# Decays by pairs of heads, gate products and k's decay on VectorE, smaller steps and longer stand-in matmuls in a linear-attention mixer with a feed-forward network

## The chip, the core and the metric

The kernel runs on one core of a Trainium2 chip. The metric is the time of one execution in microseconds (us) on the device. Shorter is better.

## The reference, cut to what matters

One decoder layer is computed: a gated linear attention mixer and then a gated feed-forward network with a causal convolution, each modulated by a conditioning vector c and followed by a residual and a layer norm. There are 2048 tokens, a width of 1024 and 2816 hidden units. Everything is float32.

```python
def post_norm_residual(x, cs, w_mod, b_mod, ln_gain, ln_bias, sublayer):
    shift, scale, gate = jnp.split((cs @ w_mod + b_mod)[:, None, :], 3, axis=-1)
    y = sublayer(x * (1 + scale) + shift)
    return layer_norm(DN_ALPHA * x + (1 + gate) * y, ln_gain, ln_bias)

# gla_mixer: 4 heads, keys 128 wide, values 256 wide, chunks of 64 tokens
    q, k, v, r, a_lr = split(h @ w_in)
    log_a = jax.nn.log_sigmoid(a_lr @ w_a2 + b_a) / GLA_TAU
    bcum = jnp.cumsum(chunks(log_a), axis=3)
    q_dec = qf * jnp.exp(bcum)
    k_inv = kf * jnp.exp(-bcum)
    k_dec = kf * jnp.exp(blast - bcum)
    att = jnp.where(causal, einsum(q_dec, k_inv), 0.0)
    o = einsum(att, vf) + q_dec @ state
    state = state * exp(blast) + einsum(k_dec, vf)
    return (rms_norm(o) * norm_g * jax.nn.silu(r)) @ w_o
```

## The kernel before, in words

**Products.** A float32 product is made of three TensorE matmuls in a reduced format: operands are split into a high part (a cast on ScalarE, line 104) and a low part (a subtraction on VectorE, line 107), and mm3 (lines 109 to 112) multiplies high by high, high by low and low by high. Weights come from memory as raw (512 KB), are split into hl, and hl is what TensorE reads.

**Mixer.** It goes over four blocks of 512 tokens. A block has 32 units of weights: 0 to 3 are v for heads 0 and 1; 4 to 7 are Q and K of heads 0 and 1; 8 to 11 r; 12 to 15 v for heads 2 and 3; 16 to 19 their Q and K; 20 to 23 r; 24 to 27 and 28 to 31 the two halves of the output projection. After each unit tick() runs what at_unit has put down for it: head_a to head_d (transposes of k, attention matrix, states, output of a head), and the preparation of the next block: its tokens (make_xm at unit 25, which modulates xraw at line 361 and splits it to xm), its low-rank decay input A3 (unit 28) and its decays (unit 29).

**Decays.** decays() makes for every head E1 and E2, the exponentials of the cumulated decays and of their negatives, through abs, exp and log on ScalarE and mn (lines 465, 468) and a scan (469) on VectorE. It needs another table of functions on ScalarE than silu does, so it begins with a table load (line 452), and the next silu (line 624) with another. gemm_q multiplies q by E1 (598 to 600), gemm_k multiplies k by E2 (611), splits KI (613) and then multiplies KI32 in place by el on GpSimd (616), which gives k for the state; TensorE transposes that at line 633.

**Gate.** The gate of the mixer's residual, G1, is a vector of 1024 that depends on c. gate_step adds one eighth of it (line 269, an instruction over 128 x 1024), gate_end finishes it. In blocks 0 and 1 the output projection's raw weights are multiplied by G1 (fold_G1, line 373, on GpSimd), in eight products a block, before they are split; the products are then kept in memory for the later blocks. The modulation for the feed-forward network (mod_cols(1, ...), lines 226 and 231, instructions over 128 x 512 on mraw) is made in block 0 too, two quarters of a group per step; mod2 (437 to 439) finishes it.

**End of a block.** out_proj accumulates four tiles of tokens in four banks of PSUM; z (line 746) evacuates each with the residual, and the next matmuls of that bank wait for it.

**Beginning.** TensorE first runs 32 stand-in matmuls on constants (spin, line 397), then sums up products for the modulation of the mixer's input: mod_cols adds rows 0 to 5 of c's matrix on VectorE (macc), ScalarE makes rows 6 and 7 (mpart, line 239), TensorE sums over partitions (242 and 257), more stand-ins come in between (2 and 9), and the result md (258) modulates the first tokens. ScalarE also begins the sum for the second group (line 224).

**Order.** All engines work through queues in order. Which instruction stands where is decided by a scheduler when the kernel is built, from the order of the program and its buffers; order(later, earlier) adds a constraint. All large loads are issued from one queue (SP) in order.

## Time and profile before

| | |
|---|---|
| time, median of 3 runs | 2188.53 us (2188.11 to 2189.34) |
| the profiled execution's own time | 2188.48 us |
| its span, first to last instruction | 2186.6 us |
| TensorE busy with matmuls | 2140.0 us, 98% |
| VectorE busy | 1447.3 us, 66% |
| ScalarE busy | 874.0 us, 40% |
| GpSimd busy | 191.0 us, 9% |
| mean granted clock of TensorE | 0.991 |

TensorE fills nearly the whole span. What it doesn't fill is 46.6 us; a matmul at a lower clock counts as busy, so a stretch at half the clock hides further time. The mixer takes about the first 870 us, the feed-forward network the rest.

### The profile page before, as it was taken

What the parts mean: (1) busy time and instruction counts of PE and PEld (TensorE: products, weight loads), DVE (VectorE), ACT (ScalarE), POOL (GpSimd) and SP (SyncE); (2) the same over time, 40 slices, a digit from 0 to 9 for tenths busy, and PEclk for the clock granted to TensorE, in tenths of its full rate; (3) what the DMA queues carried; (4) which work ended last, traced back from release to release, by engine and by line L of the source; (5) the groups of instructions that cost most, each with busy time, mean ns of one, the idle gap of its engine ahead of it and who ended that gap; (6) DMA issues with size and microseconds to landing.
All of it is one profiled execution on the core that took longest, in us unless ns stands there. A gap on an engine that the chain in (4) does not pass through costs nothing.

```text
span 2186.6 us, 26742 instructions
## 1 busy us (share of the span) xinstructions
PE 2140.0 (98%) x9891; PEld 1780.0 (81%) x9891; DVE 1447.3 (66%) x1998; ACT 874.0 (40%) x1326; POOL 191.0 (9%) x346
## 2 busy tenths in 40 slices
PE   8999899999999999999999999999999999999998
PEld 7788688877887888778888888888888888888887
DVE  6868864576445423688777779766666697578556
ACT  3634442353333223454444446333333443344333
POOL 0103311231010001100000000000000000011002
PEclk9999999999999999999999999999999999999999
DMA  7378357578746644688554559877777897577562
GB/s 295 135 245 294 116 202 258 187 282 346 284 182 221 237 159 174 256 323 319 188 190 171 187 184 319 313 268 260 263 256 268 273 321 283 183 240 268 193 202 87
DMA packets 150211, 515.66 MB, mean 236 GB/s; under 512 B 17120, under 2 KB 17248, under 8 KB 132160
## 3 DMA queue, kind: packets, MB, share of 16 engines
q1 hardware_dynamic: 150080, 513.94, 66.2%
q8 instruction: 78, 1.28, 0.2%
q14 instruction: 53, 0.43, 0.1%
HBM read 351.09 MB, written 162.79 MB: 235 GB/s over the span
## 4 chain that ended last, share of the span: by engine, by line
PE 86%; DVE 6%; DMA 3%; issue 2%; ACT 2%; POOL 1%; SPq 0%; DVEq 0%; POOLq 0%; ACTq 0%
PE ps_mm L110 21%; PE ps_mm L112 21%; PE ps_mm L111 20%; PE ps_w L111 7%; PE ps_w L110 7%; PE ps_w L112 7%; DMA raw<-in_wab_dram 1%; DVE macc L231 1%; DVE hl L107 1%; DVE az L469 1%; ACT hl L104 1%; PE ps_w L716 1%; DVE xm L107 0%; PE ps_w L757 0%; DVE xraw L361 0%
## 5 line engine op out<-in xcount | busy, mean ns | idle before, releaser
L110 PE MATMUL ps_mm<-xc,hl 128*128 128x512 f32 x704 | 274.3, 390 | 1.6 <-ACT p L945 0.8
L112 PE MATMUL ps_mm<-xc,hl 128*128 128x512 f32 x704 | 274.0, 389 | 0.2 <-DVE hl L107 0.2
L111 PE MATMUL ps_mm<-xc,hl 128*128 128x512 f32 x704 | 273.8, 389 | 0.0
L110 PE MATMUL ps_mm<-xm,hl 128*128 128x512 f32 x496 | 196.0, 395 | 0.0
L112 PE MATMUL ps_mm<-xm,hl 128*128 128x512 f32 x496 | 193.8, 391 | 0.4 <-DVE hl L107 0.4
L111 PE MATMUL ps_mm<-xm,hl 128*128 128x512 f32 x496 | 194.0, 391 | 0.0
L110 PEld LDWEIGHTS ps_mm<-xc,hl 128*128 128x128 f32 x704 | 132.1, 188 | 30.0 <-ACT p L945 1.5
L112 PEld LDWEIGHTS ps_mm<-xc,hl 128*128 128x128 f32 x704 | 132.1, 188 | 27.9 <-DVE hl L107 0.6
L111 PEld LDWEIGHTS ps_mm<-xc,hl 128*128 128x128 f32 x704 | 132.1, 188 | 27.4
L107 DVE TENSOR_TENSOR hl<-raw,hl 128x1024 fp32r<-128x1024 f32 (+1 forms) x91 | 107.9, 1187 | 68.0 <-ACT hl L104 67.6
L959 DVE SCALAR_TENSOR_TENSOR ct<-U,cw_sb,ct 128x512 f32<-128x512 f32 x176 | 131.7, 748 | 19.2 <-ACT ct L953 17.7
L104 ACT CAST hl<-raw 128x1024 fp32r<-128x1024 f32 (+1 forms) x91 | 89.3, 982 | 135.0 <-PE ps_mm L112 64.7
L110 PE MATMUL ps_w<-xc,hl 128*128 128x512 f32 x352 | 136.9, 389 | 0.0
L111 PE MATMUL ps_w<-xc,hl 128*128 128x512 f32 x352 | 136.9, 389 | 0.0
L112 PE MATMUL ps_w<-xc,hl 128*128 128x512 f32 x352 | 136.9, 389 | 0.0
L104 ACT CAST dhl<-raw 128x1024 fp32r<-128x1024 f32 x57 | 60.0, 1053 | 163.7 <-PE ps_mm L112 101.0
L107 DVE TENSOR_TENSOR dhl<-raw,dhl 128x1024 fp32r<-128x1024 f32 x57 | 69.6, 1222 | 69.2 <-ACT dhl L104 69.1
L110 PE MATMUL ps_mm<-hl,gated 128*128 128x512 f32 x256 | 101.9, 398 | 8.5 <-DVE z L746 8.5
L112 PEld LDWEIGHTS ps_mm<-xm,hl 128*128 128x128 f32 x496 | 93.4, 188 | 20.3 <-DVE hl L107 0.6
L110 PEld LDWEIGHTS ps_mm<-xm,hl 128*128 128x128 f32 x496 | 93.7, 189 | 19.0 <-DVE v L107 0.4
L111 PEld LDWEIGHTS ps_mm<-xm,hl 128*128 128x128 f32 x496 | 93.6, 189 | 18.1 <-issue 0.2
L110 PE MATMUL ps_mm<-hl,xm 128*128 128x512 f32 x256 | 100.6, 394 | 4.0 <-DVE z L746 4.0
(239 smaller groups left out, 5014.0 us busy)
## 6 DMA issues: line engine op xcount, KB each, us to landing
hl<-wq_d SPq DMA_DIRECT2D x64, 1024.0 KB, 4.8
hc_d<-ct SPq DMA_DIRECT2D x154, 256.0 KB, 2.5
raw<-hc_d SPq DMA_DIRECT2D x70, 512.0 KB, 4.3
draw<-wc_d SPq DMA_DIRECT2D x70, 512.0 KB, 4.6
raw<-in_wab_dram SPq DMA_DIRECT2D x64, 512.0 KB, 4.8
wq_d<-hl SPq DMA_DIRECT2D x32, 1024.0 KB, 4.9
wu<-in_wup_dram SPq DMA_DIRECT2D x44, 512.0 KB, 4.3
wg<-in_wup_dram SPq DMA_DIRECT2D x44, 512.0 KB, 3.7
```

The source lines that it names most:

```text
L104: accs["copy"] = nc.scalar.copy(h, src)
L107: return nc.vector.tensor_tensor(l, src if lsrc is None else lsrc, h.bitcast(F32), op=ALU.subtract)
L110: nc.tensor.matmul(po, a[0], b[0], start=first, stop=False, skip_group_check=resumed)
L111: nc.tensor.matmul(po, a[0], b[1], start=False, stop=False, skip_group_check=resumed)
L112: return nc.tensor.matmul(po, a[1], b[0], start=False, stop=last, skip_group_check=resumed)
L231: accs["last"] = nc.vector.scalar_tensor_tensor(acc, wk, sc, acc, op0=ALU.mult, op1=ALU.add)
L469: nc.vector.tensor_tensor_scan(az, smask, mn, 0.0, op0=ALU.mult, op1=ALU.add)
L716: nc.tensor.transpose(pt[:, s * P:s * P + P], on[:, s, e * P:e * P + P], ident)
L959: nc.vector.scalar_tensor_tensor(ct, U[:, o + i:o + i + 512], cw_sb[:, j, i:i + 1], ct, op0=ALU.mult, op1=ALU.add)
```

## The change

- **Beginning:** 62, 4 and 18 stand-ins instead of 32, 2 and 9. VectorE adds rows 0 to 6, and only row 7 is ScalarE's. The first three raw weights are loaded between the other transfers of the beginning instead of behind them.
- **Gate product and k's decay:** fold_G1 is a VectorE instruction; k's decay is one VectorE instruction over 128 x 512 with el as a broadcast operand, instead of two GpSimd instructions over 128 x 256.
- **Decays:** heads 0 and 1 at unit 29 of the block before (at the beginning for block 0), heads 2 and 3 at unit 12 of the block itself. E1 and E2 have 4 buffers instead of 8, A3 has a buffer of its own. There are eight more table loads: 16 behind the first one of the kernel where there were 8.
- **Steps:** gate steps of block 0 one unit earlier and each behind the latest split of weights; mod_cols(1, ...) in 16 steps of one quarter at units 14 to 24 instead of eight steps of two at 17 to 24.

Lines from 266 on move by one to three: 361, 373, 437, 598, 611, 746 become 362, 374, 440, 601, 614, 748, and k's decay is 618.

```diff
-SPIN = (32, 2, 9)
+SPIN = (62, 4, 18)
...
         if dk == 0:
-            nc.vector.tensor_scalar(acc, raw, cs[:, 0:1], None, op0=ALU.mult)
+            i = nc.vector.tensor_scalar(acc, raw, cs[:, 0:1], None, op0=ALU.mult)
         else:
-            nc.vector.scalar_tensor_tensor(acc, raw, cs[:, dk:dk + 1], acc, op0=ALU.mult, op1=ALU.add)
+            i = nc.vector.scalar_tensor_tensor(acc, raw, cs[:, dk:dk + 1], acc, op0=ALU.mult, op1=ALU.add)
+        order(i, accs["hl"])
...
             def f(raw):
                 rv = raw.rearrange("p (k c) -> p k c", k=2)
                 g = G1[:, None, half * 512:half * 512 + 512].to_broadcast([P, 2, 512])
-                nc.gpsimd.tensor_tensor(rv, rv, g, op=ALU.mult)
+                nc.vector.tensor_tensor(rv, rv, g, op=ALU.mult)
...
                 mod_load(w[q], 0, pr, q)
+            if pr == 0:
+                load_unit()
             xr = z_tile("xraw")
...
         start_loads(0)
+        load_unit()
         war = t2p.tile([P, KT, 16], F32, tag="t2", name="war")
         load(war, wa)
-        for n in range(3):
-            load_unit()
+        load_unit()
         start_loads(1)
...
-        mod_cols(0, 0, range(4), start[0][0], rows=range(6))
+        mod_cols(0, 0, range(4), start[0][0], rows=range(7))
         acc_last = accs["last"]
-        spin(SPIN[1], pm0, mod_rows_act(start[0][0], (6, 7), pm0))
+        spin(SPIN[1], pm0, mod_rows_act(start[0][0], (7,), pm0))
...
-        def decays(A3):
+        def decays(A3, heads):
...
-            for h in range(NH):
+            for h in heads:
...
-                E1 = ab.tile([P, TB], F32, tag="E", name="E1", bufs=8)
-                E2 = ab.tile([P, TB], F32, tag="E", name="E2", bufs=8)
+                E1 = ab.tile([P, TB], F32, tag="E", name="E1", bufs=4)
+                E2 = ab.tile([P, TB], F32, tag="E", name="E2", bufs=4)
...
-            for c in range(2):
-                nc.gpsimd.tensor_tensor(kk[:, :, c], kk[:, :, c],
-                                        el[:, 1 + c, :, None].to_broadcast([P, 4, CH]), op=ALU.mult)
+            nc.vector.tensor_tensor(kk, kk, el[:, 1:3].rearrange("p c s -> p s c")[:, :, :, None].to_broadcast([P, 4, 2, CH]),
+                                    op=ALU.mult)
...
+            at_unit(b + 12, next_decays, (2, 3))
             if tb == 0:
                 load(lnc, lncol)
                 for k in range(8):
-                    at_unit(9 + k, gate_step, 0, k, gs1)
-                at_unit(17, gate_end, 0, G1, gs1)
-                for i in range(KT):
-                    at_unit(17 + i, mod_cols, 1, i // 2, (i % 2 * 2, i % 2 * 2 + 1))
-                    if i % 2:
-                        at_unit(18 + i, mod_fin, 1, i // 2)
+                    at_unit(8 + k, gate_step, 0, k, gs1)
+                at_unit(16, gate_end, 0, G1, gs1)
+                for i, u in enumerate((14, 14, 15, 15, 16, 16, 16, 17, 17, 18, 19, 20, 21, 22, 23, 24)):
+                    at_unit(u, mod_cols, 1, i // 4, (i % 4,))
+                    if i % 4 == 3:
+                        at_unit(u + 1, mod_fin, 1, i // 4)
...
-                at_unit(b + 29, next_decays)
+                at_unit(b + 29, next_decays, (0, 1))
```

**Where instructions move, on VectorE.** A row is line, operation, what is written and read, shape, and how often in a row; numbers in names are buffers. First the queue ahead of the first decay of k (KI_793) in block 0. Before, up to the split of that KI, behind which GpSimd multiplied:

```order
L465 TENSOR_SCALAR mn<-ps_w,ba_sb 128x512
L599 SCALAR_TENSOR_TENSOR Q_786<-ps_w,E_724 128x4x64
L107 TENSOR_TENSOR hl<-raw,hl 128x1024
L600 TENSOR_TENSOR Q_786<-Q_786,el 128x4x64
L465 TENSOR_SCALAR mn<-ps_w,ba_sb 128x512
L468 TENSOR_TENSOR mn<-mn,az 128x512
L611 TENSOR_TENSOR KI_793<-ps_w,E_725 128x512
L469 SCALAR_TENSOR_TENSOR az<-smask,mn 128x512
L468 TENSOR_TENSOR mn<-mn,az 128x512
L107 TENSOR_TENSOR Q<-Q_786,Q 128x768
L469 SCALAR_TENSOR_TENSOR az<-smask,mn 128x512
L107 TENSOR_TENSOR KI<-KI_793,KI 128x512
```

And with the change, up to the product itself:

```order
L107 TENSOR_TENSOR hl<-raw,hl 128x1024
L471 TENSOR_TENSOR mn<-mn,az 128x512
L601 SCALAR_TENSOR_TENSOR Q_786<-ps_w,E_760 128x4x64
L472 SCALAR_TENSOR_TENSOR az<-smask,mn 128x512
L602 SCALAR_TENSOR_TENSOR Q_786<-ps_w,E_760 128x4x64
L614 TENSOR_TENSOR KI_793<-ps_w,E_761 128x512
L603 TENSOR_TENSOR Q_786<-Q_786,el 128x4x64
L107 TENSOR_TENSOR hl<-raw,hl 128x1024
L107 TENSOR_TENSOR Q<-Q_786,Q 128x768
L107 TENSOR_TENSOR KI<-KI_793,KI 128x512
L601 SCALAR_TENSOR_TENSOR Q_829<-ps_mm,E_778 128x4x64
L618 TENSOR_TENSOR KI_793<-KI_793,el 128x512
```

Of heads 2 and 3 the mn, subtractions and scans (465, 468, 469) have left this place, and the product is the last row. On TensorE 58 matmuls of the projections stand between the decays' matmuls and the transposes of that KI, where there were 71.

Next the queue ahead of the first z of block 0. Before, z is the row before the last:

```order
L258 TENSOR_TENSOR md<-ps_w,mbs_sb 128x4
L107 TENSOR_TENSOR xm<-xraw,xm 128x512
L361 TENSOR_SCALAR xraw<-xraw,md 128x512 x3
L107 TENSOR_TENSOR xm<-xraw,xm 128x512 x3
L361 TENSOR_SCALAR xraw<-xraw,md 128x512 x2
L437 TENSOR_TENSOR A_106<-lnc,md 128x8
L438 TENSOR_TENSOR B_107<-lnc,md 128x8
L439 TENSOR_TENSOR B_107<-B_107,md 128x8
L107 TENSOR_TENSOR hl<-raw,hl 128x1024
L107 TENSOR_TENSOR xm<-xraw,xm 128x512 x2
L746 SCALAR_TENSOR_TENSOR z<-z,ps_mm 128x512
L107 TENSOR_TENSOR hl<-raw,hl 128x1024
```

With the change z is the last row:

```order
L107 TENSOR_TENSOR xm<-xraw,xm 128x512
L362 TENSOR_SCALAR xraw<-xraw,md 128x512 x2
L374 TENSOR_TENSOR raw<-raw,G_279 128x1024
L107 TENSOR_TENSOR xm<-xraw,xm 128x512 x2
L107 TENSOR_TENSOR hl<-raw,hl 128x1024
L440 TENSOR_TENSOR A_106<-lnc,md 128x8
L441 TENSOR_TENSOR B_107<-lnc,md 128x8
L374 TENSOR_TENSOR raw<-raw,G_279 128x1024
L442 TENSOR_TENSOR B_107<-B_107,md 128x8
L374 TENSOR_TENSOR raw<-raw,G_279 128x1024
L107 TENSOR_TENSOR hl<-raw,hl 128x1024
L748 SCALAR_TENSOR_TENSOR z<-z,ps_mm 128x512 x4
```

Between the last sr and these rows stand one modulation of xraw (362), two gated, five xm and one md. Three gate products (374; raw with G) have come into VectorE's own queue ahead of z, the last xm have moved ahead of the last split of weights, and the four z are one group now.

Last the queue in block 2 where xp, a difference of tokens for the feed-forward network, falls among Q and KI of heads 0 and 1. Before, up to the splitting of the first KI:

```order
L289 TENSOR_TENSOR xp<-xp 128x1024
L611 TENSOR_TENSOR KI_4578<-ps_mm,E_4124 128x512
L289 TENSOR_TENSOR xp<-xp 128x1024 x2
L598 SCALAR_TENSOR_TENSOR Q_4616<-ps_mm,E_4141 128x4x64
L289 TENSOR_TENSOR xp<-xp 128x1024
L107 TENSOR_TENSOR KI<-KI_4578,KI 128x512
L599 SCALAR_TENSOR_TENSOR Q_4616<-ps_mm,E_4141 128x4x64
```

With the change, up to the decay of that k:

```order
L107 TENSOR_TENSOR Q<-Q_4518,Q 128x768
L614 TENSOR_TENSOR KI_4572<-ps_mm,E_4154 128x512
L290 TENSOR_TENSOR xp<-xp 128x1024 x4
L601 SCALAR_TENSOR_TENSOR Q_4609<-ps_mm,E_4171 128x4x64
L602 SCALAR_TENSOR_TENSOR Q_4609<-ps_mm,E_4171 128x4x64
L107 TENSOR_TENSOR hl<-raw,hl 128x1024
L107 TENSOR_TENSOR KI<-KI_4572,KI 128x512
L603 TENSOR_TENSOR Q_4609<-Q_4609,el 128x4x64
L618 TENSOR_TENSOR KI_4572<-KI_4572,el 128x512
```

All four xp stand together now, a split of weights (hl) and the rest of Q come ahead of KI's split, and the decay follows in the same queue.

## Rows read from the trace of the kernel before

**Rows 1.** Busy time by engine in stretches of the run. Columns: the stretch and its length; busy time of PE (matmuls), PEld (weight loads), DVE, ACT and POOL with the number of instructions; the granted clock; the DMA engines' busy share; GB/s.

```profile
160.00:240.00 80.00, 69.83 (x354) 59.42 (x354) 71.12 (x106) 31.80 (x65) 25.85 (x18) 0.95 0.77 262
...
1000.00:2000.00 1000.00, 1000.00 (x4413) 827.87 (x4412) 740.90 (x947) 411.93 (x531) 36.27 (x90) 1.00 0.71 249
```

**Rows 2.** Who waited for whom on TensorE, over the whole run: total, times, longest.

```profile
PE ps_mm L110 <- DVE z L746: 12.5, 7, 6.9
...
PE ps_w L633 <- POOL KI L616: 9.6, 3, 4.7
...
PE ps_w L110 <- DVE S L676: 1.6, 1, 1.6
...
PE ps_w L111 <- DVE Shl L107: 1.5, 1, 1.5
```

**Rows 3.** Busy time and granted clock in a microsecond of the first stand-ins and in the five stretches at 0.5. Columns as in rows 1.

```profile
6.40:7.40 1.00, 1.00 (x11) 1.00 (x9) 0.95 (x2) 0.00 (x0) 0.00 (x0) 1.00 1.07 412
...
9.75:19.99 10.24, 9.19 (x38) 8.52 (x39) 3.54 (x7) 5.05 (x8) 0.00 (x0) 0.50 1.04 412
...
88.25:95.08 6.83, 6.39 (x23) 5.71 (x24) 6.72 (x12) 4.41 (x7) 0.39 (x1) 0.50 0.45 147
...
177.00:180.41 3.41, 3.41 (x18) 3.41 (x17) 3.32 (x8) 1.89 (x5) 0.00 (x0) 0.50 1.01 311
...
235.03:241.85 6.82, 5.22 (x12) 4.13 (x13) 6.78 (x9) 1.05 (x1) 2.37 (x1) 0.50 0.66 231
...
531.99:538.81 6.82, 5.22 (x25) 5.22 (x26) 4.67 (x11) 3.10 (x5) 1.36 (x2) 0.50 0.98 371
```

**Rows 4.** Instructions of the beginning, TensorE's and then VectorE's first step for the modulation: start, length, line, what is written and read, shape, how many; in brackets the idle time ahead and who ended it.

```profile
1.38 6.27 PE L397 MATMUL ps_w<-still 128*128 128x256 f32 x32 [1.38 <-DVE still L165]
...
10.26 3.76 PE L242 MATMUL ps_w<-ones,mpart 128*128 128x1 f32 x16 [2.61 <-ACT mpart L239]
...
14.91 1.87 PE L257 MATMUL ps_w<-ones,macc 128*128 128x1 f32 x8 [0.26 <-DVE md L253]
...
21.89 0.50 PE L112 MATMUL ps_w<-xm,hl 128*128 128x512 f32 x1 [0.34 <-DVE hl L107]
...
5.64 0.49 DVE L226 TENSOR_SCALAR macc<-mraw,cs 128x512 f32<-128x512 f32 x1 [2.18 <-DMA mraw<-in_mws_dram]
```

**Rows 5.** GpSimd's gate products and decays of k, grouped by line: how many, busy time, mean of one in ns, and the idle time ahead of them by who ended it.

```profile
L373 POOL TENSOR_TENSOR raw<-raw,G 128x1024 f32<-128x1024 f32 x16 | 42.1, 2640 | 70.3 <-DMA raw<-in_wab_dram 42.5 <-DVE xm L107 12.4 <-DMA xraw<-in_xT_dram 7.8
...
L616 POOL TENSOR_TENSOR KI<-KI,el 128x256 f32<-128x256 f32 x32 | 20.0, 644 | 300.6 <-DVE KI L107 300.5
```

**Rows 6.** VectorE's instructions grouped by line and shape, columns as in rows 5: two element-wise products and sums of the feed-forward network in the shapes of a gate product (with a broadcast operand G) and of k's decay, and the three operations of the decays.

```profile
L878 DVE TENSOR_TENSOR wd<-wd,G 128x1024 f32<-128x1024 f32 x22 | 26.8, 1220 | 2.1 <-DMA wd<-in_wdn_dram 2.0
...
L878 DVE TENSOR_TENSOR ct<-ct 128x512 f32<-128x512 f32 x88 | 60.7, 689 | 22.3 <-DMA hc_d<-ct 21.0
...
L465 DVE TENSOR_SCALAR mn<-ps_w,ba_sb 128x512 f32<-128x512 f32 x16 | 11.9, 746 | 10.3 <-ACT az L461 10.0
...
L468 DVE TENSOR_TENSOR mn<-mn,az 128x512 f32<-128x512 f32 x16 | 10.9, 679 | 0.0
...
L469 DVE TENSOR_TENSOR_SCAN az<-smask,mn 128x512 f32<-128x512 f32 x16 | 19.5, 1217 | 0.2
```

**Rows 7.** Instructions around the first decays of k in block 0: TensorE's transposes of heads 0 and 1, VectorE's second mn, and GpSimd's product for head 1.

```profile
82.35 0.66 PE L633 MATMUL ps_w<-ident,KI 128*128 128x128 f32 x4 [2.35 <-POOL KI L616]
...
88.69 1.11 PE L633 MATMUL ps_w<-ident,KI 128*128 128x128 f32 x4 [2.60 <-POOL KI L616]
...
66.30 0.75 DVE L465 TENSOR_SCALAR mn<-ps_w,ba_sb 128x512 f32<-128x512 f32 x1 [0.96 <-ACT az L461]
...
87.40 1.23 POOL L616 TENSOR_TENSOR KI<-KI,el 128x256 f32<-128x256 f32 x2 [4.76 <-DVE KI L107]
```

**Rows 8.** Instructions at the end of block 0, VectorE's and then the first matmul of the output projection's second half.

```profile
189.97 2.01 DVE L231 SCALAR_TENSOR_TENSOR macc<-mraw,cs,macc 128x512 f32<-128x512 f32 x1 [0.28 <-DMA mraw<-in_mws_dram]
...
195.08 2.50 DVE L231 SCALAR_TENSOR_TENSOR macc<-mraw,cs,macc 128x512 f32<-128x512 f32 x1
...
217.02 1.23 DVE L107 TENSOR_TENSOR hl<-raw,hl 128x1024 fp32r<-128x1024 f32 x1 [3.15 <-ACT hl L104]
...
225.78 5.25 DVE L361 TENSOR_SCALAR xraw<-xraw,md 128x512 f32<-128x512 f32 x2
...
230.95 2.31 DVE L437 TENSOR_TENSOR A<-lnc,md 128x8 f32<-128x8 f32 x1
...
235.80 0.68 DVE L746 SCALAR_TENSOR_TENSOR z<-z,ps_mm 128x512 f32<-128x512 f32 x1
...
239.33 3.73 DVE L107 TENSOR_TENSOR hl<-raw,hl 128x1024 fp32r<-128x1024 f32 x2
...
236.63 0.76 PE L110 MATMUL ps_mm<-hl,gated 128*128 128x512 f32 x1 [6.93 <-DVE z L746]
```

**Rows 9.** Instructions in block 2, where xp stands among Q and KI: VectorE's and then GpSimd's product.

```profile
527.40 2.49 DVE L289 TENSOR_TENSOR xp<-xp 128x1024 f32<-128x1024 f32 x2 [1.41 <-DMA xp<-xm_d]
...
531.40 0.69 DVE L107 TENSOR_TENSOR KI<-KI,KI 128x512 fp32r<-128x512 f32 x1
...
532.18 1.36 POOL L616 TENSOR_TENSOR KI<-KI,el 128x256 f32<-128x256 f32 x2 [35.17 <-DVE KI L107]
```

**Rows 10.** The table loads of the decays on ScalarE, grouped by line, columns as in rows 5.

```profile
L452 ACT ACT_TABLE_LOAD x4 | 5.1, 1283 | 0.1
```

More of the change, by code (lines that the diff above doesn't have):

```diff
@@ L454, in decays @@
                 order(ld, silu_done[-1])
-            res = []
-            for h in range(NH):
+            res = {}
+            for h in heads:
                 lg = psum("w", 4)
@@ L461, in decays @@
                 i0 = nc.scalar.activation(az, lg, AF.Abs, bias=bah)
-                if h == 0:
+                if h == heads[0]:
                     order(ld, i0)
@@ L478, in decays @@
                 nc.gpsimd.tensor_tensor(el[:, 1], el[:, 0], el[:, 2], op=ALU.mult)
-                res.append((E1, E2, el))
+                res[h] = E1, E2, el
             return res
@@ L487, in evac_a @@
         def evac_a(pa):
-            A3 = t2p.tile([96, TB], F32R, tag="t2", name="A3")
+            A3 = ab.tile([96, TB], F32R, tag="A3", name="A3")
             nc.scalar.copy(A3, pa[0:96])
@@ L547, in gemm_start @@
                 v_part(banks, pr, xm)
-            accs.clear()
+            del accs["last"]
             ahead[0] = AHEAD
@@ L776, in normalise @@
             nc.scalar.activation(z, z, AF.Identity, bias=rs[:, 1:2], scale=rs[:, 0:1])
-        nxt = {}
+        nxt = {"E": {}}
         def next_xm(tb):
@@ L784, in next_a, with next_decays @@
             nxt["A3"] = gemm_a(nxt["xm"])
-        def next_decays():
-            nxt["E"] = decays(nxt["A3"])
+        def next_decays(heads):
+            nxt["E"].update(decays(nxt["A3"], heads))
         gs1, gs2 = {}, {}
@@ L829 @@
                 at_unit(b + 28, next_a)
-                at_unit(b + 29, next_decays)
+                at_unit(b + 29, next_decays, (0, 1))
             pqk = {}
             if tb == 0:
-                xm, A3, v0, pqk["pq"], pqk["pk"] = gemm_start()
-                nxt["E"] = decays(A3)
+                xm, nxt["A3"], v0, pqk["pq"], pqk["pk"] = gemm_start()
+                next_decays((0, 1))
             else:
                 v0 = gemm_v(xm, tick)
-            E = nxt["E"]
             for pr in range(2):
                 v = v0 if pr == 0 else gemm_v(xm, tick)
+                E = nxt["E"]
                 for h in (2 * pr, 2 * pr + 1):
```

## Prediction

> **What bounds the kernel now.** I read the stretches first. In the feed-forward network TensorE is busy in all 1000 of 1000 us, while VectorE has 741 and ScalarE 412 [rows 1]. Nothing in that part changes, so whatever is gained or lost before it is carried to the end unaltered. In the last 80 us of the first token block it is the other way round: VectorE 71.1 of 80, TensorE 69.8 [rows 1]. What can be won is TensorE's idle time in the mixer, so I read its waits next: 12.5 us for z (the evacuation of the output projection), the longest 6.9; 9.6 us for KI (k's decay on GpSimd) in three waits, the longest 4.7; 1.6 for S; 1.5 for Shl [rows 2]. Then the granted clock. Behind four of these places, and at the beginning, it stands at 0.5, which is the lower level (1.2 GHz) [rows 3]. TensorE was busy there for 6.39, 3.41, 5.22 and 5.22 us; the same work takes half of that at the full clock, so these stretches cost 3.2, 1.7, 2.6 and 2.6 us over the waits themselves. Last I read the single instructions at each wait.
>
> So the avoidable time that the change touches, by place:
> - First heads of block 0: waits of 2.35 and 2.60 [rows 7] + 3.2 = 8.2.
> - S and Shl behind the gate and modulation steps of block 0: 1.6 + 1.7 + 1.5 = 4.8.
> - End of block 0: 6.93 + 2.6 = 9.5.
> - The six other waits for z, 12.5 - 6.9 = 5.6.
> - Heads 0 and 1 of block 2: 4.7 + 2.6 = 7.3.
>
> Together 35.4 us, and the beginning besides.
>
> **The change part by part.** The sum is made against the profiled execution's own 2188.48 us (span 2186.6), which is 0.05 under the median of the runs.
>
> *Beginning.* The 32 stand-in matmuls run from 1.38 to 7.65, TensorE then waits 2.61 us for mpart, and from 9.75 on the clock is at 0.5 [rows 3, 4]. The 16 one-column products and 8 more behind them therefore take 3.76 and 1.87 us [rows 4]. Thirty more stand-ins at 11 in a microsecond [rows 3] reach to about 10.4, and half of the mpart products go. At the full clock that half needs a quarter of 3.76 and macc's products half of 1.87, 0.94 each, so with the short steps between them the modulation stands at about 13.5 and not 16.98. That isn't all passed on. ScalarE's queue has L224 ahead of the cast for k's weights, and L224 needs the first mraw of the second group. It is the ninth large transfer; the first landed at 5.6 [rows 4], and at 412 GB/s [rows 3] each 0.52 MB takes 1.27 us, so it lands at about 15.9 whatever TensorE does. From there L224 0.7, cast 1.0 and subtraction 1.2 give 18.8, where the matmul that waits for it started at 21.89 [rows 4]. Value: -3.0. Bounds: 0, if the loads that follow, which come at the same pace, set the end of this stage; -4, if ScalarE is ahead.
>
> *Gate product on VectorE.* On GpSimd one takes 2.64 us [rows 5]. VectorE does the same shape with a broadcast operand in 1.22 [rows 6]. While GpSimd worked, VectorE's own instructions grew: in block 0 six of them, the first a step of 2.01 instead of 0.75 us and the last a pair of splits of 3.73 instead of 2.4, the largest two of L361, 5.25 instead of 1.0 [rows 8]; 12.9 us in all by differences to the same rows unhindered. Eight products cost 8 x 1.14 (start to start) = 9.1 there. So VectorE's load in this block falls by only 3.8 us: what matters is where the pieces stand. The Trainium skill ("SBUF — State Buffer", section "SBUF: two separate sides") says that GpSimd and a VectorE instruction with two operands in SBUF exclude each other for the whole instruction. By it VectorE would have lost up to GpSimd's whole 8 x 2.64 = 21.1 us, the gain would be 8.2 greater, and the time 2155.5. The trace agrees that they exclude each other, but the instructions that read PSUM beside a gate product were not longer; I take the 12.9.
>
> *End of block 0.* Before, z began at 235.80 and TensorE, ready at 229.70, started at 236.63 [rows 8]. Ahead of z VectorE waited 3.15 us for ScalarE and then worked from 217.02 on, with 6.4 us of lengthening in two rows [rows 8]. In the new order, 13.4 us of work stand between the last sr (ends 213.9) and z: 2 gated, 8 xm, 3 xraw, 3 gate products, 2 hl and four tiny ones, at 0.60, 0.60, 0.46, 1.14, 1.14 and 0.07 from start to start. z is free to start at about 227.5, before TensorE needs it. Value -9.0 (0.5 kept for a small wait). Bounds: 0 if the products wait for their weights (below), -9.5.
>
> *First heads of block 0.* Six operations for heads 2 and 3 leave VectorE's queue: 2 x (0.75 + 0.68 + 1.22) = 5.3 us [rows 6]. From the second mn at 66.30 [rows 7] the new order has 10.5 us of work to the end of k's decay, which itself is 0.69 for a pair of products of that size [rows 6] instead of two at 0.64 on another engine [rows 5]: 76.8, with some waiting for ScalarE 78.2. TensorE was ready at 80.0 (82.35 less the wait of 2.35), but has 58 and not 71 matmuls of the projections before the transposes, 13 x 0.226 us less, so it is ready at 77.1 and waits 1.1. Behind it I count 0.1 for the next transposes, 1.3 and 0.6 for S and Shl, and 0.9 for the clock: 4.0 left of 8.2. Value -4.1 (0 to -8.2).
>
> *S and Shl.* The steps of two quarters become steps of one, in units 14 to 24, and no GpSimd product doubles a step in front of Shl (195.08: 2.50 us [rows 8]). By durations the new queue has 47.6 us of work in this stretch and TensorE 47.2, which is tight; 1.0 of 4.8 stays. Value -3.8 (0 to -4.8).
>
> *Other waits for z.* In blocks 1 to 3 two heads' decays, not four, stand among the evacuations, and no GpSimd product beside them. 2.2 of 5.6 stays. Value -3.4 (0 to -5.6).
>
> *Block 2.* Before, KI's split started at 531.40 behind two xp subtractions that waited for a DMA until 527.40, and GpSimd's 1.36 us followed [rows 9]. Now four xp stand together, and then 598, 599, hl, KI's split, 600 and the decay: from 527.40, 3 x 1.13 + 0.68 + 1.14 + 0.60 + 0.34 + 0.60 = 6.8, so 534.2. TensorE gets nine more matmuls first and is ready at 528.9 + 2.0 = 530.9. The wait is still 3.3, and the clock probably falls again. Value -2.0 (0 to -7.3).
>
> *New costs.* Eight more table loads at 1.283 us [rows 10] are 10.3 us of ScalarE, which is busy in 31.8 of the 80 us of the busiest stretch [rows 1]; its casts feed VectorE, so I put 0.5 on the path (0 to 10.3). The Trainium skill ("ScalarE: Activation LUTs", section "Table sets: the hidden batching unit") speaks against the pairs: calls are to be batched by set, and a load with its drain is about 2.7 us. Eight would be 21 us by it; the rows show 0.1 us of idling before four of them, so the drain isn't seen here. The E buffers, four instead of eight, are free again before unit 12, since heads 0 and 1 used them up in units 4 to 8; nothing.
>
> Sum: -3.0 - 9.0 - 4.1 - 3.8 - 3.4 - 2.0 + 0.5 = -24.8, so 2188.5 - 24.8 = 2163.7, say 2164.
>
> **The rivals.**
> 1. *VectorE stays the bound in block 0.* Its load falls by only 3.8 us there, and 47.6 against 47.2 is no margin. Then z waits at the end of block 0 for 6, not 0.5 (+5.5 and the clock's 2.6 back), S and Shl keep 3.8, and the first heads 2: 24.8 - 13.9 = 10.9, so 2177.6, in a span of 2172 to 2184. For it: 71.1 of 80 us busy. Against: 6.4 us of lengthening directly ahead of z are gone.
> 2. *Table loads on the path.* All eight: 2163.7 + 9.8 = 2173.5. Against: ScalarE's 40%.
> 3. *Every touched wait goes*, the beginning too: 35.4 + 3.0 = 38.4, so 2150.
> 4. *No change*: each stall is replaced by another in the same stage, because what TensorE gains early is spent at the next evacuation; 2184 to 2193.
> 5. *Slower: the gate products wait in VectorE's queue.* GpSimd sat idle for 42.5 us until the raw weights of these products had landed [rows 5], and nobody stood behind it. VectorE's queue is in order: whoever waits there holds up Q, KI, gated and z. If all of it came on the path, 2188.5 - 24.8 + 42.5 = 2206. It decides from 24.8 us on. For it: 8.9 us of slack in those 80 us [rows 1] don't cover it. Against: the new order puts the products behind xraw rows whose loads are issued in the same queue after those weights, so the weights are mostly there.
>
> **Numbers.** A time within 0.2% (4.4 us) of before can't be told from it. Forecast (2153 to 2172) 0.57; rival 1 0.18; rival 2 0.03; rival 3 0.08; no change 0.06; slower 0.08. Faster: 0.57 + 0.18 + 0.03 + 0.08 = 0.86. The range must leave out no more than 0.2: it takes the forecast, rival 2, about seven tenths of rival 1 (to 2181) and most of rival 3 (from 2148): 0.57 + 0.03 + 0.13 + 0.07 = 0.80.
>
> **What the changed profile would show.** The first real matmul by about 16 and the clock at 1.0 from 2 to 20; waits for z of about 2.7 us in all with none over 1 at the end of block 0; waits for KI, now with VectorE as releaser, of about 1 in block 0 and 3 in block 2; the 0.5 clock left in block 2 and perhaps once in block 0; L373's work on VectorE at about 1.2 us each, and the stretch 1000 to 2000 as full as before. I am wrong if the gate products have idle time for raw before them with TensorE waiting behind, if z still waits over 3 us at the end of block 0, or if the sum of the mixer's waits falls by less than 10.

## Result, and the profile after

The changed kernel takes 2163.24 us (median; 2159.95 to 2164.01) beside 2188.94 for the kernel before: a ratio of 0.988, 95% interval 0.9863 to 0.9897. That is 25.7 us faster, and 0.8 us from the forecast of 2164. The sum came out; several of its terms did not, and their errors cancelled. The profiled execution took 2164.01 us.

The page's busy line, and the two stretches of [rows 1] in the changed kernel, columns as there:

```profile
PE 2135.5 (99%) x9924; PEld 1780.3 (82%) x9924; DVE 1456.6 (67%) x2031; ACT 886.2 (41%) x1333; POOL 134.5 (6%) x298
```

```profile
160.00:240.00 80.00, 78.15 (x402) 66.64 (x402) 68.51 (x110) 37.54 (x71) 6.06 (x8) 0.98 0.74 260
...
1000.00:2000.00 1000.00, 999.53 (x4410) 827.23 (x4409) 732.62 (x931) 408.90 (x524) 35.07 (x88) 1.00 0.70 247
```

From 160 to 240 us, which was the end of block 0 before, TensorE works 78.15 instead of 69.8 us, VectorE 68.5 instead of 71.1 and GpSimd 6.1 instead of 25.9. The feed-forward network is as full as it was.

TensorE's waits over the whole run, which answer [rows 2]:

```profile
PE ps_w L110 <- DVE S L678: 6.5, 3, 3.0
...
PE ps_mm L112 <- DVE hl L107: 1.8, 2, 1.6
...
PE ps_w L635 <- DVE KI L618: 0.9, 1, 0.9
```

No wait for z is left where there were seven, and the three for KI (9.6 us) have become one of 0.9. Waits for S have grown from 1.6 to 6.5 us, and one of 1.6 us for the low half of weights (hl) has come in block 2, where TensorE had waited 4.7 us for KI: at these two places a new stall took part of an old one's place.

How far ahead the changed kernel is shows where the same matmul (the n-th of its kind) starts in both traces:

| matmul, and the stage that ends there | before | after | ahead | in this stage | forecast |
|---|---|---|---|---|---|
| 54th of v in block 0: the beginning | 48.82 | 48.49 | 0.33 | 0.3 | 3.0 |
| 16th of v and KTt: first heads of block 0 | 101.89 | 101.18 | 0.71 | 0.4 | 4.1 |
| 8th of the output projection: S and Shl, block 0 | 207.51 | 205.38 | 2.13 | 1.4 | 3.8 |
| 126th of it: end of block 0 | 249.44 | 237.68 | 11.76 | 9.6 | 9.0 |
| 735th with xm: to the end of block 1 | 515.59 | 495.98 | 19.61 | 7.9 | about 2.6 |
| 111th of v and KTt: heads 0 and 1 of block 2 | 561.24 | 537.00 | 24.24 | 4.6 | 2.0 |
| 75th transpose of z: end of block 2 | 724.96 | 698.92 | 26.04 | 1.8 | about 0.8 |
| 253rd with xc: feed-forward network | 1016.93 | 991.94 | 24.99 | -1.0 | -0.5 |

The forecast's 3.4 us for the other waits for z are split here by where those waits stood: 1.3 of the 5.6 us at the end of block 2, the rest earlier. By stage, the first three were 8.8 us too optimistic together, and the three from block 1 on 8.9 us too careful.

*Beginning.* TensorE's stand-ins and the first real matmul, then the instruction that finishes the modulation, which answer [rows 4]:

```profile
1.38 10.21 PE L400 MATMUL ps_w<-still 128*128 128x256 f32 x62 [1.38 <-DVE mhalf L167]
...
14.66 4.21 PE L400 MATMUL ps_w<-still 128*128 128x256 f32 x18 [0.26 <-DVE md L258]
...
18.66 0.63 PE L110 MATMUL ps_w<-xm,hl 128*128 128x512 f32 x1
...
14.44 0.16 DVE L258 TENSOR_TENSOR md<-ps_w,md 128x4 f32<-128x4 f32 x1 [1.28 <-PE ps_w L257]
```

The modulation is there at 14.44 instead of 16.82 us. Then 18 stand-ins take 4.21 us, and the first matmul starts at 18.66 where it had been 19.12. Two stretches of TensorE, columns: length, busy time, granted clock, DMA share and GB/s:

```profile
16.00:18.00 2.00, 2.00 (x11) 0.50 1.06 410
...
90.00:92.00 2.00, 1.80 (x8) 0.50 0.43 168
```

The first of them stands for the stretch from about 14 to 20.8 us: the clock was at 0.5 in this execution, as in [rows 3], although TensorE had run stand-ins for 10.2 us and was idle after them only for two steps of 0.26 us, with 16 one-column products and 4 stand-ins between.

*First heads of block 0.* VectorE's queue, ScalarE's, and TensorE's two waits:

```profile
84.63 1.22 DVE L107 TENSOR_TENSOR hl<-raw,hl 128x1024 fp32r<-128x1024 f32 x1
...
85.76 0.47 DVE L678 SCALAR_TENSOR_TENSOR S<-S,el,ps_w 128x256 f32<-128x256 f32 x1
...
86.16 1.28 DVE L269 SCALAR_TENSOR_TENSOR gacc<-graw,cs,gacc 128x1024 f32<-128x1024 f32 x1
...
87.87 0.48 DVE L678 SCALAR_TENSOR_TENSOR S<-S,el,ps_w 128x256 f32<-128x256 f32 x1
...
89.58 0.47 DVE L678 SCALAR_TENSOR_TENSOR S<-S,el,ps_w 128x256 f32<-128x256 f32 x1
...
86.70 1.28 ACT L626 ACT_TABLE_LOAD   x1
...
88.48 0.40 ACT L104 CAST Shl<-S 128x256 fp32r<-128x256 f32 x1
...
86.29 0.35 PE L110 MATMUL ps_w<-Q,KI 128*128 128x192 f32 x1 [1.71 <-DVE S L678]
...
90.20 0.55 PE L110 MATMUL ps_w<-v,at 128*128 128x256 f32 x1 [2.99 <-DVE S L678]
```

What TensorE waits for are the PSUM banks that hold the new contributions to S. An update of S (678) frees its part, but S is updated in place: the next update waits until both halves of the last have been split off, the cast on ScalarE and the subtraction (Shl) on VectorE. Between them stand a split of weights (84.63), a gate step (86.16) and on ScalarE a table load (86.70) with a silu behind it, so that the cast of the state of 87.87 starts at 88.48. The four updates take from 82.8 to 90.05. The clock falls at the end of it and stands at 0.5 from 89.1 to 95.9 us, with 5.7 us of matmuls in it, so half of that, 2.9 us by estimate, is lost besides. Before, TensorE spent this time waiting for KI.

*End of block 0.* VectorE's instructions ahead of z, and the gate products grouped by line, which answer [rows 8] and [rows 5]:

```profile
213.09 3.09 DVE L107 TENSOR_TENSOR xm<-xraw,xm 128x512 fp32r<-128x512 f32 x5
...
218.14 1.22 DVE L374 TENSOR_TENSOR raw<-raw,G 128x1024 f32<-128x1024 f32 x1
...
225.34 1.88 DVE L748 SCALAR_TENSOR_TENSOR z<-z,ps_mm 128x512 f32<-128x512 f32 x3
...
227.60 0.69 DVE L748 SCALAR_TENSOR_TENSOR z<-z,ps_mm 128x512 f32<-128x512 f32 x1 [0.38 <-PE ps_mm L112]
...
L374 DVE TENSOR_TENSOR raw<-raw,G 128x1024 f32<-128x1024 f32 x16 | 19.3, 1220 | 1.6 <-DMA raw<-in_wab_dram 1.6
```

z starts at 225.34 with TensorE still at work on the first half (the fourth z waits 0.38 us for TensorE). Before, z was 10.5 us later (235.80). The products take 1.22 us each, and in all sixteen VectorE waited 1.6 us for raw weights where GpSimd had waited 42.5.

*Block 2.* The loading queue's issues around xp, first in the kernel before and then with the change, followed by VectorE's xp and its first decay of k, which answer [rows 9]:

```profile
515.30 1.14 SPq L283 DMA_DIRECT2D xp<-xm_d  x2
...
521.22 0.32 SPq L144 DMA_DIRECT2D wq_d<-hl  x1
...
521.65 1.34 SPq L283 DMA_DIRECT2D xp<-xm_d  x2
```

```profile
495.90 3.48 SPq L284 DMA_DIRECT2D xp<-xm_d  x4
...
499.43 0.55 SPq L125 DMA_DIRECT2D raw<-in_wab_dram  x1
...
504.50 5.00 DVE L290 TENSOR_TENSOR xp<-xp 128x1024 f32<-128x1024 f32 x4
...
512.15 0.68 DVE L618 TENSOR_TENSOR KI<-KI,el 128x512 f32<-128x512 f32 x1
```

Before, two loads of xp stood behind a store of split weights (521.22) that had to wait for the split; with the change all four are issued at 495.90 and nothing waits for them on VectorE.

### The profile page after: what moved, and what is told of

It is laid out like the page before. It is cut to its first block, busy times and chain, and to the rows that moved or that the text cites. A ratio compares the mean times of both kernels' runs of the same rounds, so it can differ in the third digit from the quotient of the medians.

```text
span 2162.3 us, 26743 instructions
## 1 busy us (share of the span) xinstructions
PE 2135.5 (99%) x9924; PEld 1780.3 (82%) x9924; DVE 1456.6 (67%) x2031; ACT 886.2 (41%) x1333; POOL 134.5 (6%) x298
## 4 chain that ended last, share of the span: by engine, by line
PE 92%; DVE 3%; ACT 2%; DMA 2%; issue 1%; POOL 0%; SPq 0%; DVEq 0%; POOLq 0%; ACTq 0%
PE ps_mm L110 22%; PE ps_mm L112 22%; PE ps_mm L111 22%; PE ps_w L110 8%; PE ps_w L111 8%; PE ps_w L112 8%; DMA xs<-xt_d 1%; PE ps_w L400 1%; PE ps_w L718 1%; DMA raw<-in_wab_dram 1%; PE ps_w L759 0%; DVE hl L107 0%; PE ps_w L487 0%; ACT hl L104 0%; PE ps_w L488 0%
## 5 line engine op out<-in xcount | busy, mean ns | idle before, releaser
L107 DVE TENSOR_TENSOR hl<-raw,hl 128x1024 fp32r<-128x1024 f32 (+1 forms) x91 | 103.4, 1138 | 56.7 <-ACT hl L104 56.2
L110 PE MATMUL ps_mm<-dhl 128*128 128x512 f32 x264 | 102.7, 389 | 0.0
L111 PE MATMUL ps_mm<-dhl 128*128 128x512 f32 x264 | 102.7, 389 | 0.0
```

The lines of the kernel that those rows point to most:

```text
L107: return nc.vector.tensor_tensor(l, src if lsrc is None else lsrc, h.bitcast(F32), op=ALU.subtract)
L110: nc.tensor.matmul(po, a[0], b[0], start=first, stop=False, skip_group_check=resumed)
L111: nc.tensor.matmul(po, a[0], b[1], start=False, stop=False, skip_group_check=resumed)
```

## Experiments

**e1: the gate product alone back on GpSimd.**

```diff
-                nc.vector.tensor_tensor(rv, rv, g, op=ALU.mult)
+                nc.gpsimd.tensor_tensor(rv, rv, g, op=ALU.mult)
```

> The changed kernel with the gate product alone back on GpSimd. Theory A, the gate products on VectorE are what took the wait for z away at the end of block 0: that wait comes back at 5 to 7 us, with the lower clock behind it another 2 to 3, and waits for z in block 1 too, so about 2173 (2170 to 2176). Theory B, it was the order of the other steps (modulation of the second layer finished earlier, decays in pairs), and the product itself only changes hands: z waits under 2 us at the end of block 0 and the time is 2162 to 2167.

2174.39 us (2174.04 to 2176.58), ratio 0.9929 (0.9914 to 0.9943): theory A. Its waits for z, and VectorE's and GpSimd's longest instructions ahead of them:

```profile
PE ps_mm L110 <- DVE z L748: 6.2, 3, 3.0
...
222.09 2.39 DVE L442 TENSOR_TENSOR B<-B,md 128x8 f32<-128x8 f32 x1
...
225.58 6.16 DVE L107 TENSOR_TENSOR hl<-raw,hl 128x1024 fp32r<-128x1024 f32 x2 [0.49 <-ACT hl L104]
...
222.06 11.90 POOL L374 TENSOR_TENSOR raw<-raw,G 128x1024 f32<-128x1024 f32 x4 [14.30 <-DVE B L441]
```

Four products come together just there. An operation of 8 columns takes 2.39 us instead of 0.16, and two splits of 1.2 us take 6.16; GpSimd too is held up (11.90 us for four, 2.4 each elsewhere in this trace). Of the three waits for z two stand at the end of block 0 (3.0 and 1.6 us, where before had 6.9) and one at the end of block 1 (1.6), where four products again take 12.19 us; there are none in the later blocks, which have no such products. By the stages of the table above, the end of block 0 takes 37.7 us instead of the changed kernel's 32.3 and the stage behind it 261.8 instead of 258.3. The lower clock that theory A expected behind z did not come.

**e2: k's decay alone back on GpSimd.**

```diff
-            nc.vector.tensor_tensor(kk, kk, el[:, 1:3].rearrange("p c s -> p s c")[:, :, :, None].to_broadcast([P, 4, 2, CH]),
-                                    op=ALU.mult)
+            for c in range(2):
+                nc.gpsimd.tensor_tensor(kk[:, :, c], kk[:, :, c],
+                                        el[:, 1 + c, :, None].to_broadcast([P, 4, CH]), op=ALU.mult)
```

> The changed kernel with k's decay alone back on GpSimd, as two instructions. Theory A, GpSimd's place behind VectorE's split was the cause of the waits for KI: the wait of the first head of block 0 grows from 0.9 to 2 to 3 us, one of 1 to 3 us comes back in block 2, the time is 2166 to 2170. Theory B, the waits for KI went because other work left VectorE's queue and xp's loads came in time: no wait for KI over 2 us, none in block 2, and 2161 to 2165.

2163.87 us (2163.40 to 2164.51), ratio 0.9879 (0.9864 to 0.9893): theory B, but for 0.6 us of a wait for KI that stays in block 2.

```profile
PE ps_w L636 <- POOL KI L619: 3.2, 3, 1.9
```

All waits for KI together are 3.2 us, spread over three heads, and the one for S in the first heads is shorter instead (3.0 against 4.7), that of the third head longer (2.9 against 1.9). Where k's decay is made makes no difference that can be measured.

**e3: the decays of four heads at one place again** (8 buffers for E1 and E2, A3 as before).

```diff
-            at_unit(b + 12, next_decays, (2, 3))
...
-                at_unit(b + 29, next_decays, (0, 1))
+                at_unit(b + 29, next_decays, (0, 1, 2, 3))
...
-                next_decays((0, 1))
+                next_decays((0, 1, 2, 3))
```

> The changed kernel with the decays of all four heads at one place again, with 8 buffers for E1 and E2 and nine table loads. Theory A, the decays of heads 2 and 3 among the evacuations are what z waited for in blocks 1 to 3: waits for z of 4 to 6 us in all come back there, and 2 to 5 us of waits for KI in block 0, so 2170 to 2175. Theory B, z was held up by the gate products on GpSimd alone: no wait for z over 0.5 us after block 1, and 2161 to 2166.

2174.63 us (2173.95 to 2175.86), ratio 0.9928 (0.9913 to 0.9943): as dear as theory A said, but about half of it by something that neither theory named. Its longest waits, and its loading queue in block 2:

```profile
PE ps_mm L110 <- ACT hl L104: 5.2, 1, 5.2
...
PE ps_mm L110 <- DVE z L748: 2.8, 3, 1.3
...
PE ps_mm L111 <- DVE hl L107: 1.5, 1, 1.5
...
PE ps_mm L112 <- DVE hl L107: 1.4, 1, 1.4
...
505.79 0.32 SPq L144 DMA_DIRECT2D wq_d<-hl  x1
...
506.21 2.61 SPq L284 DMA_DIRECT2D xp<-xm_d  x3
...
508.87 0.77 SPq L125 DMA_DIRECT2D raw<-in_wab_dram  x1
```

Only 2.8 us of waits for z come back, and 1.5 us for a low half of weights (at 473 us), ahead of which a subtraction and a scan of the decays (469.59 and 470.87) stand in VectorE's queue. In block 0 nothing is lost: the first heads wait for KI 1.4 us and the 126th matmul of the output projection starts at 235.15, earlier than in the changed kernel (237.68, and 236.34 in e12). In block 2 three loads of xp wait behind a store (505.79), the next load of weights (508.87) behind them, and TensorE waits 5.2 us for the cast of these weights and 1.4 more for their low half. By the stages of the table, and beside e12, the two stages in which z had waited take 5.5 and 1.8 us longer and heads 0 and 1 of block 2 6.5 us.

**e4: gate steps and modulation in the steps of before.**

```diff
-        order(i, accs["hl"])
...
-                    at_unit(8 + k, gate_step, 0, k, gs1)
-                at_unit(16, gate_end, 0, G1, gs1)
+                    at_unit(9 + k, gate_step, 0, k, gs1)
+                at_unit(17, gate_end, 0, G1, gs1)
...
-                    at_unit(u, mod_cols, 1, i // 4, (i % 4,))
+                    at_unit(17 + i, mod_cols, 1, i // 2, (i % 2 * 2, i % 2 * 2 + 1))
```

> The changed kernel with the gate steps of block 0 one unit later again, without their order behind a split, and the second layer's modulation in eight steps of two quarters. Theory A, the gate step that moved ahead sits in VectorE's queue between the updates of S and makes the new waits for S at the first heads (4.7 us and the lower clock behind): these shrink by 2 to 5 us, and in return the steps of two quarters bring back 1 to 3 us at S, Shl and z later in block 0: 2160 to 2165. Theory B, S's own chain of updates and splits makes those waits: they stay within 1 us of 4.7, and the time is 2164 to 2168.

2163.90 us (2158.63 to 2165.63), ratio 0.9873 (0.9857 to 0.989). The waits of the first heads between 60 and 100 us:

```profile
PE ps_w L110 <- DVE KTt L107: 2.6, 1, 2.6
...
PE ps_w L110 <- DVE S L677: 2.2, 1, 2.2
```

The wait for S shrinks by 2.5 us as theory A said, but KTt takes 2.6: 4.8 us of waits where there were 4.7. No gain or loss can be measured from the steps.

**e5: the beginning of before.**

```diff
-SPIN = (62, 4, 18)
+SPIN = (32, 2, 9)
...
-        mod_cols(0, 0, range(4), start[0][0], rows=range(7))
+        mod_cols(0, 0, range(4), start[0][0], rows=range(6))
```

> The changed kernel with the beginning of before (32, 2 and 9 stand-ins, rows 6 and 7 on ScalarE, the first raw weights loaded last). Theory A, the longer stand-ins keep the clock at its upper level through the first matmuls in most executions, which is worth the 1.5 to 2.5 us that four profiles show 50 us into the run: about 2165 (2164 to 2166). Theory B, the loads set the end of this stage and the beginning is worth nothing, as the profile of the changed kernel itself shows it (0.3): 2163, within 1 us. In its trace the clock stands at 0.5 from about 10 to 20 either way.

2164.30 us (2162.27 to 2166.62), ratio 0.9884 (0.9869 to 0.9899); the clock is at 0.5 from about 10 to 20 us. It lies in theory A's range and 0.3 us outside theory B's, but can't be told from the changed kernel, so neither theory is shown. Its profile is 1.4 us behind the kernel before at 50 us, and in the second half of block 0's output projection just where the changed kernel's first profile is (11.75 and 11.76 ahead).

**e6: gate steps two units later than the change has them.**

```diff
-                    at_unit(8 + k, gate_step, 0, k, gs1)
-                at_unit(16, gate_end, 0, G1, gs1)
+                    at_unit(10 + k, gate_step, 0, k, gs1)
+                at_unit(18, gate_end, 0, G1, gs1)
```

> The changed kernel with the gate steps of block 0 two units later (units 10 to 17, end at 18). In the built order no gate step is left between the updates of S for heads 0 and 1. Theory A, the gate steps there make the waits for S (4.7 us) and so also the lower clock that follows them (about 3): both go, and with nothing lost later the time is 2155 to 2159. Theory B, the split of weights and the chain of S itself make them: waits of 3 to 5 us stay between 80 and 95 us, 2162 to 2165. What could be lost later: the steps come together with the decays of heads 2 and 3 and the modulation, 1 to 3 us of waits for S at the third head.

2162.58 us (2160.76 to 2164.04), ratio 0.9875 (0.9861 to 0.989). The waits of the first heads, the longest one later in block 0, and a stretch of TensorE:

```profile
PE ps_w L110 <- DVE S L678: 4.2, 2, 3.0
...
PE ps_w L277 <- DVE KTt L107: 2.1, 1, 2.1
...
76.00:90.00 14.00, 9.84 (x58) 0.88 0.11 37
```

Without a gate step among the updates the waits for S are still 4.2 us: theory B. The clock fell here too, but for a shorter time: the last row is TensorE from 76 to 90 us at a mean of 0.88, with 0.5 from 86.4 to 89.8. Later 2.1 us were lost again.

**e8: two parts of the change alone on the kernel before**, the gate products on VectorE and the decays by pairs.

```diff
-                nc.gpsimd.tensor_tensor(rv, rv, g, op=ALU.mult)
+                nc.vector.tensor_tensor(rv, rv, g, op=ALU.mult)
...
-                at_unit(b + 29, next_decays)
+                at_unit(b + 29, next_decays, (0, 1))
...
+            at_unit(b + 12, next_decays, (2, 3))
```

> The kernel before with two parts of the change alone: the gate products on VectorE and the decays by pairs of heads; k's decay, the steps and the beginning are as before. If these two carry the gain (each undone by itself cost 11 us, k's decay and the steps 1 or less), it takes 2164 to 2168: the beginning's 1 to 2 us are missing. If the parts only work together, with k's decay or the steps needed for the end of block 0, it takes 2172 to 2180.

2163.44 us (2160.07 to 2166.39), ratio 0.9879 (0.9865 to 0.9894): the whole gain, with the other three parts left out, and 0.6 us under what the first case of the expectation allowed.

**e9: the kernel before, with xp in block 2 put down one unit earlier.**

```diff
-                at_unit(b + 4, x_pre, 0, 0)
+                at_unit(b + 3, x_pre, 0, 0)
```

> The kernel before with one edit: the preparation of xp in block 2 is put down one unit earlier. In the built order its four loads then stand together in the loading queue, where two of them had stood behind a store that waits for a split of weights. Theory A, that place in the loading queue made the wait for KI in block 2 (4.7 us, and the lower clock behind, 2.6): it shrinks to under 1 us and the time is 2181 to 2184. Theory B, VectorE's own work or GpSimd's product made it: a wait of 3 to 5 us for KI stays in block 2, 2187 to 2190.

2191.11 us (2189.33 to 2192.53), ratio 1.0005 (0.9996 to 1.0015). Its waits in the stretch from 420 to 600 us, the load of weights behind xp, and the cast of these weights:

```profile
PE ps_mm L110 <- ACT hl L104: 4.7, 2, 3.4
...
PE ps_mm L112 <- DVE hl L107: 1.5, 2, 1.1
...
519.32 0.42 SPq L125 DMA_DIRECT2D raw<-in_wab_dram  x1
...
524.82 1.05 ACT L104 CAST hl<-raw 128x1024 fp32r<-128x1024 f32 x1 [5.60 <-DMA raw<-in_wab_dram]
```

No wait for KI is left in block 2, as theory A said, but the time is that of before. The load of weights now stands behind xp's loads (519.32), the cast waits for it until 524.82, and TensorE 3.4 us for the cast and 1.1 for the low half; with 1.7 us for the weights behind them it is 6.2 us, all in block 2.

**e10: two buffers for S in turn.**

```diff
-        S32 = ab.tile([P, NH, DV], F32, name="S32")
+        S32 = [ab.tile([P, NH, DV], F32, name=f"S32{i}") for i in range(2)]
+        turn_s = [0] * NH
...
-                        nc.vector.scalar_tensor_tensor(S32[:, h], S32[:, h], el[:, 1, s:s + 1], po,
+                        old = S32[turn_s[h]][:, h]
+                        turn_s[h] = 1 - turn_s[h]
+                        nc.vector.scalar_tensor_tensor(S32[turn_s[h]][:, h], old, el[:, 1, s:s + 1], po,
```

> The changed kernel with two buffers for the state S, used in turn, so that an update of S no longer waits until both halves of the one before are split off. Theory A, the chain update - cast - subtraction - next update (four times per head, the cast once behind a table load and a silu on ScalarE) holds the PSUM banks that TensorE waits for: the waits for S at the first heads shrink from 4.7 to 1 to 2 us, that of the third head (1.9) too, and the clock falls there less often: 2156 to 2160. Theory B, the gate steps and the split of weights between the updates hold the banks: they still stand there, the waits stay over 3.5, and the time is within 2 us of 2163.

2157.48 us (2155.76 to 2158.49), ratio 0.9854 (0.9838 to 0.9871): the fastest kernel here, 5.0 us under the changed kernel in the same comparison (e12). Its waits for S from 60 to 100 us, and its wait for KTt from 100 to 200:

```profile
PE ps_w L110 <- DVE S L681: 3.2, 2, 2.6
...
PE ps_w L110 <- DVE KTt L107: 1.5, 1, 1.5
```

The time is as theory A had it, the waits only in part. That for S at the third head is gone, with 1.5 us for KTt in its place; at the first heads 3.2 us stay, and the split of weights and the gate step still stand between the updates (theory B's part). Nor is the whole gain that of the chain: beside e12's profile this one is 0.7 us ahead behind the first heads, 3.7 at the 8th matmul of the output projection, 2.8 at the end of block 1 and 5.5 behind heads 0 and 1 of block 2. Between the last two of these the loading queue has changed with the build: in e10 a split of weights is done (491.28) before xp's loads are issued (491.67), where in e12 the load of weights stands behind them (498.05), and the wait for a low half (1.6 us in e12) is gone.

**e11: two buffers as in e10, and the gate steps two units later as in e6.**

```diff
-                    at_unit(8 + k, gate_step, 0, k, gs1)
+                    at_unit(10 + k, gate_step, 0, k, gs1)
...
+        S32 = [ab.tile([P, NH, DV], F32, name=f"S32{i}") for i in range(2)]
```

> The same two buffers for S, and the gate steps of block 0 two units later, so that neither stands in the chain. If the chain and the steps each hold part of the banks' time, the waits for S at the first heads fall under 1 us and the time is 2154 to 2158; what is then left at heads 2 and 3 are the waits for KTt that the later gate steps brought (2.1 and 1.2 us). If the waits only move on to KTt or to the attention matrices, it is no better than with the two buffers alone.

2157.62 us (2154.48 to 2160.89), ratio 0.9853 (0.9839 to 0.9868). Between 60 and 100 us:

```profile
PE ps_w L110 <- DVE KTt L107: 1.9, 1, 1.9
...
PE ps_w L110 <- DVE S L681: 1.7, 2, 1.0
```

The wait for S falls to 1.7 us and moves on to KTt, as the second case of the expectation had it; the sum, 3.6, is not less than e10's 3.2.

**e12: the changed kernel again.** No edit.

> The changed kernel once more beside these two, for a comparison on one chip: 2163 within 2 us. If the beginning's clock is the difference among its executions, this profile shows the clock at 1.0 from 12 to 20 us and the matmuls 50 us into the run 1.5 to 2.5 us earlier than before, where the first profile had 0.3.

2162.52 us (2162.17 to 2163.44), ratio 0.9876 (0.9862 to 0.9891). The stretch from 16 to 18 us, columns as above:

```profile
16.00:18.00 2.00, 2.00 (x14) 1.00 1.08 414
```

Here the clock held, the first matmul came at 16.68, 2.0 us earlier than in the first profile, and at 48 us the lead over before is 2.4 us instead of 0.3.

## Why the prediction was right, point by point

**What bounds the kernel: right.** All gain is ahead of the feed-forward network, which carries it through.

**End of block 0: right, -9.6 measured for -9.0.** The products cost 1.22 us each, z starts before TensorE needs it, and no wait is left. e1 shows the other side: with the products on GpSimd the longest instructions on VectorE are again those beside a product, and this stage is 5.4 us longer. The other 4.2 us of the 9.6 are gained in e1 too. The Trainium skill ("SBUF — State Buffer", section "SBUF: two separate sides") says of GpSimd and a VectorE instruction with two operands in SBUF that whichever starts first blocks the other for its whole length. My estimate by that rule was a gain 8.2 us larger. The measured 25.7 us are nearer to the 24.8 of the rows than to 33.0, but as errors of other terms cancelled, this does not decide between the two.

**Other waits for z: the step was right, the size too small.** I kept 2.2 us of 5.6; none stayed. e1 and e3 divide them: with the products on GpSimd one of 1.6 us comes back (end of block 1), with four heads together three of 2.8 us in all. With 5.6 us of waits gone, 7.9 and 1.8 us were gained in the two stages that hold them. Of the difference, 0.9 us are two waits in the heads of block 1 (0.3 for KTt, 0.5 for the attention matrix) that are gone too; the rest was not followed up.

**Block 2: the term failed in its mechanism.** I read VectorE's new order and a DMA that landed at 527.40, and took that landing as given. It was not: it hung on the loading queue, in which two loads stood behind a store. The order of that queue had changed too, and I had not looked at it there. e3 and e9 show what this queue does: either xp or the weights come late, depending on which stands behind the other, and in e3 behind a store. The waits sum to 4.7 us for xp's case and to more than 6 in e3 and e9; in the changed kernel 1.6 us for weights is left. Why the pairs bring the queue into the better order is not shown step by step; e3 shows that without them it isn't there.

**First heads: the step that failed** is "1.3 and 0.6 for S and Shl". The waits for KI went as forecast (0.9 left, 1.1 said). But I had not followed S's chain: four updates in place, each waiting for a cast on another engine. It lay under the wait for KI, as I read it. It takes 4.7 us where I had 1.9 for S and Shl, and the low clock 2.9 where I had 0.9. What holds the banks is shown in part: the second buffer (e10) takes 1.5 us of the 4.7 away, later gate steps (e6) 0.5, and both together (e11) leave 3.6 us, half of it for KTt, no less than e10's 3.2. What makes the rest is open. A table load with its silu stands in the chain, which is rival 2's mechanism at one place, though no run took it out by itself. The eight additional loads are 10.3 us of ScalarE and did not cost the 10 us of rival 2; e3, without them, was slower. The decays' loads with the change, of which four are new (the other four new ones are silu's):

```profile
L455 ACT ACT_TABLE_LOAD x8 | 10.3, 1283 | 0.1
```

**S and Shl: -1.4 for -3.8.** The wait for Shl went, the one for S at the third head (1.9 us here, 3.3 in e12, 1.6 before) didn't, nor the lower clock behind it; e10 has no wait for S there, but one for KTt. By e4 the smaller steps have no measurable part in it. The 47.6 and 47.2 us of work that I set against each other stand without their terms, and no run shows them.

**Beginning: -3.0 was the value of one state of the clock.** At 48 us the change is 0.3 us ahead where the clock fell and 1.7 to 3.0 in the other profiles with the same beginning. The old beginning varies as much: its four profiles (before, e5, e8, e9) reach the same matmul between 47.65 and 50.21 us. On the average of these profiles the new one is about 2 us earlier. By e5 this is not to be told from nothing in the end; the profiles of e5 and e12 stand 3.8 us apart at 50 us and 1.4 at the end of block 0. My lower bound of 0 stands, for another reason than the one I gave.

**Slower rival: refuted.** In VectorE's queue the gate products waited 1.6 us for their weights, not 42.5: when VectorE came to them, nearly all the weights were there.

**The other rivals.** Rival 1 (VectorE stays the bound) has its mark, z, against it: no wait for z is left, though S kept waiting as it said. Rival 3 failed by S, whose waits grew. Rival 4 (every stall replaced by another) came true at the first heads alone, and by a third in block 2. Of what I said the profile would show, the first matmul by 16 us and the clock at 1.0 up to 20 came, give or take 0.7 us, in the other profiles of this beginning but not in the first, and the 0.5 clock left in block 2 did not come. The lower clock stood in four stretches before the end of block 0, where I had expected one at most.

The total within 0.8 us of the forecast is luck in part: 8.8 us too much in the first three stages and 8.9 too little in the last three.

So the whole gain lies in two of the five parts: the gate products on VectorE and the decays by pairs. Taken away alone, each costs about 11 us (e1, e3), and both together give all of it (e8). Counted from the kernel before in the same comparisons (2190.2 and 2190.4), the pairs without the products on VectorE give 15.8 us and the products without the pairs 15.5, each with the other three parts in place; the two alone give 26.9, where the whole change in its second comparison (e12) gives 27.6.

## What to carry to other kernels

When a wait is removed, follow the chain that ran beside it to its end before the gain is booked: an accumulator updated in place, whose next update waits for a copy made by another engine, holds its banks for the whole round trip; here two buffers in turn took 1.5 of 4.7 us of that wait away. Read the new order of the loading queue wherever a term rests on a landing, for here a store that waited for an engine delayed the loads behind it (521.22, and 505.79 in e3). A rebuilt kernel can change that order by itself, as e10 did, so read it before a gain is put down to the edit. A product moved off an engine that blocks another can be worth more than the load it saves: about 11 us in e1, where by the prediction's sum VectorE's load in block 0 fell by only 3.8 us.
